# Values times probabilities with a head's high and low values side by side as the weights

## The chip, the cores and the metric

The kernel runs as one program on one core of a Trainium2 chip. The metric is the device time of one execution in microseconds (us), lower is better. TensorE (PE) does the matrix products, its weight loads have rows of their own (PEld), and VectorE (DVE), ScalarE (ACT) and GpSimd (POOL) do the element-wise work. SyncE (SP) and POOL issue the transfers.

## The reference

Two transformer blocks in float32 on 512 tokens of width 1024, one after the other. Cut to the order of the stages and to the attention on which the change bears:

```python
def first_block(x, ...):                       # one layer
    x = x + 0.5 * _swiglu(_rms_norm(x), w1, w3, w2)
    proj = _rms_norm(x) @ w_in                 # q, k, v of 8 heads of 64, and HGRN2
    attn_out = _dilated_attention(aq, ak, av)  # three windows (128,1) (512,4) (2048,16)
    rec = _hgrn2(hq, hf, hi, lower_bounds)     # chunkwise recurrence, f = lb + (1-lb)*sigmoid
    x = x + concat([attn_out, rec]) @ w_out
    return x + 0.5 * _swiglu(_rms_norm(x), ...)

def hybrid_mixer(h, ...):                      # in each of two layers of the second block
    o_cmp, p_cmp = cmp_attention(q, kc_c, vc_c)            # compressed keys and values
    o_sel = sel_attention(q, ks, vs, select_blocks(p_cmp)) # 8 heads, 2 groups of values
    o_win = win_attention(q, kw, vw)
    o_attn = g[0] * o_cmp + g[1] * o_sel + g[2] * o_win
    return concat([o_attn, short_conv(u, bg, cg, conv_w)]) @ w_o

# each attention ends in  o = einsum(p, v),  p = softmax(scores)
# second block: mixer, layer_norm, swiglu (layer 0) or an 8-expert MoE (layer 1), layer_norm
```

## The kernel before

The stages run one after the other: a feed-forward (0 to 390 us), the first block's mixer `mix1` (to 730), a feed-forward (to 1110), the second block's mixer `mix2` of layer 0 (to about 1375), a feed-forward (to 1850), `mix2` of layer 1 (to about 2080) and the experts (to 2650).

To keep float32 accuracy each operand of a product is split in a high part and a low part, both of the matmul's type (helper `cut`: ACT writes the high part, L417, and DVE subtracts it to get the low one, L418). `mm3` then does three matmuls into one PSUM tile: high by high (L429), low by high (L430) and high by low (L431).

An attention unit (`unit`) is one head's scores, softmax and product with the values for all 512 queries. PE multiplies queries and keys (L943, L944), DVE and ACT do the maximum and the exponential, POOL scales the exponentials (tile `ex`, L963), PE transposes them (L975) into the tile `ps_t`, `cut` splits them (tiles `pr`), and then come the products with the values, four of them, over 512, 256, 128 and 384 queries, each an `mm3` into `hd["o"]`, a PSUM tile `ps_o` of 128 rows by 512 queries. There are 8 units in `mix1` and 16 in each of the two `mix2`. The weights of such a product are 128 columns of values, those of two heads or groups side by side. A head's own values give 64 of the 128 rows; the other 64 are not read. At a head's close (`close` in `mix1`, the compressed products L1564 in `mix2`) `cut` takes the head's 64 rows out of `ps_o` into the tiles `mix`, `nat` or `tok`. In `mix2` two units (selected and window) and the compressed product add up in the same `ps_o`, so there are 8 closes in each mixer. The operands of L1564 are the compressed probabilities and the weights `vst`.

The order of the instructions on each engine is settled when the program is built. Generators such as `unit`, `hgrn` and `finish_v` yield a PE cost and a lag at each step; the planner `flow` picks who goes next by these estimates, and mixes the attention with other products (`ps_mm<-act`: projections and the convolution's weights; `ps_mm<-tok` and `ps_s<-tok`: the output projection of heads that are closed). On the chip every engine then works through its list in that order, and waits where a semaphore is not there yet.

`clear` zeroes two buffers in DRAM, `xs` and `ys`, which the experts use much later. It runs once, in `mix1`: POOL fills a tile with zeros (L1115) and issues 13 transfers (L1119, L1125, L1129) from its own queue. `hgrn` is the recurrence; its step 1 - f runs on POOL (L1008), and DVE and PE's transposes (L1044) come after it.

## Time and profile before

| | |
|---|---|
| time, median of 3 runs (lowest to highest) | 2662.02 us (2652.87 to 2662.17) |
| the profiled execution: time / span | 2650.37 us / 2648.7 us |
| busy share of the span: PE / DVE / ACT / POOL | 95% / 61% / 45% / 36% |
| granted TensorE clock, mean | 0.974 |
| PE instructions | 14302 matmuls, 14302 weight loads |

A matmul's row has its start and a modelled length; neighbouring rows overlap, so what a matmul costs PE is the distance from its start to the next one's. A row of the timeline ends with the idle time of its engine just before it, and what ended that.

### The profile page before, as it was taken

The page shows a single profiled execution, that of the slowest core. Times are in us where ns is not written, and L with a number is a line of the kernel's source. Part 1 is how long each engine was busy: PE and PEld are TensorE (multiplying, and loading weights), DVE is VectorE, ACT ScalarE, POOL GpSimd, SP SyncE. Part 2 cuts the span into 40 slices and gives each one's busy share as a digit, 9 for nine tenths or more (in the row PEclk, how much of TensorE's full clock was granted, in tenths as well). Part 3 has the DMA queues.
Part 4 walks back from the last instruction along what each step waited for, and adds up shares of the span by engine and source line. Part 5 has one row for each costly group of instructions (what it writes and reads, how often), then busy time and mean ns, then how long its engine had stood idle before and what let it go on. Part 6 is the DMA issues. An engine that isn't in the chain of part 4 may idle for free. (4 is left out here: it accounts for less than half of the span.)

```text
span 2648.7 us, 39980 instructions
## 1 busy us (share of the span) xinstructions
PE 2515.8 (95%) x14302; PEld 2180.2 (82%) x14302; DVE 1616.7 (61%) x3288; ACT 1191.6 (45%) x2179; POOL 965.3 (36%) x939
## 2 busy tenths in 40 slices
PE   8999999969999999999999999999999698999985
PEld 7888889858888887898888888889888597979884
DVE  6434455738754344686775323358776787799876
ACT  4222245535532222365544222235554276777763
POOL 4222222423122322433233222243332336767873
PEclk9999999979899999999999999999999898999997
DMA  4232232382032322241112232233211289799981
GB/s 161 81 110 96 74 117 80 99 185 77 24 99 79 110 96 74 94 136 63 58 41 80 81 107 100 75 107 103 82 60 46 73 301 330 262 369 324 332 309 69
DMA packets 103771, 342.06 MB, mean 129 GB/s; under 512 B 11984, under 2 KB 12800, under 8 KB 103568
## 3 DMA queue, kind: packets, MB, share of 16 engines
q1 hardware_dynamic: 95472, 311.58, 34.5%
q0 software_dynamic: 8096, 27.87, 4.0%
q8 instruction: 115, 1.88, 0.3%
q14 instruction: 88, 0.72, 0.1%
HBM read 316.59 MB, written 22.81 MB: 128 GB/s over the span
## 5 line engine op out<-in xcount | busy, mean ns | idle before, releaser
L282 POOL TENSOR_TENSOR w_lo<-w_raw,w_hi 128x224 fp32r<-128x224 f32 (+2 forms) x578 | 671.3, 1168 | 1153.6 <-ACT w_hi L276 1083.3
L276 ACT CAST w_hi<-w_raw 128x1024 fp32r<-128x1024 f32 (+3 forms) x615 | 600.5, 981 | 868.8 <-issue 243.2
L280 DVE TENSOR_TENSOR w_lo<-w_raw,w_hi 128x800 fp32r<-128x800 f32 (+5 forms) x616 | 653.3, 1067 | 301.0 <-ACT w_hi L276 294.4
L430 PE MATMUL ps_mm<-act_lo,w_hi 128*128 128x512 f32 (+1 forms) x784 | 304.0, 388 | 0.7 <-DVE act_lo L418 0.7
L429 PE MATMUL ps_mm<-act_hi,w_hi 128*128 128x512 f32 (+1 forms) x784 | 304.2, 389 | 0.0
L431 PE MATMUL ps_mm<-act_hi,w_lo 128*128 128x512 f32 (+1 forms) x784 | 303.3, 387 | 0.0
L429 PE MATMUL ps_s<-act_hi,w_hi 128*128 128x512 f32 (+1 forms) x456 | 174.6, 383 | 6.8 <-ACT w_hi L279 6.8
L963 POOL TENSOR_SCALAR ex<-ex,st 128x512 f32<-128x512 f32 (+3 forms) x160 | 90.0, 574 | 233.3 <-DVE st L960 151.3
L430 PE MATMUL ps_s<-act_lo,w_hi 128*128 128x512 f32 (+1 forms) x456 | 174.1, 382 | 0.0
L431 PE MATMUL ps_s<-act_hi,w_lo 128*128 128x512 f32 (+1 forms) x456 | 173.8, 381 | 0.4 <-DVE w_lo L280 0.4
L431 PEld LDWEIGHTS ps_mm<-act_hi,w_lo 128*128 128x128 f32 x784 | 149.2, 190 | 29.4
L430 PEld LDWEIGHTS ps_mm<-act_lo,w_hi 128*128 128x128 f32 x784 | 148.8, 190 | 28.8 <-DVE act_lo L418 1.0
L429 PEld LDWEIGHTS ps_mm<-act_hi,w_hi 128*128 128x128 f32 x784 | 148.3, 189 | 28.2
L429 PE MATMUL ps_mm<-w_hi,act_hi 128*128 128x256 f32 (+1 forms) x544 | 156.5, 288 | 7.0 <-DVE nat L1252 3.2
L431 PE MATMUL ps_mm<-w_hi,act_lo 128*128 128x256 f32 (+1 forms) x544 | 155.5, 286 | 0.2 <-DVE act_lo L634 0.2
L430 PE MATMUL ps_mm<-w_lo,act_hi 128*128 128x256 f32 (+1 forms) x544 | 154.9, 285 | 0.0
L955 ACT ACTIVATE ex<-ex,st 128x512 f32<-128x512 f32 (+3 forms) x160 | 89.7, 562 | 62.7 <-DVE st L953 62.4
L429 PEld LDWEIGHTS ps_mm<-w_hi,act_hi 128*128 128x128 f32 x544 | 103.0, 189 | 8.7 <-DVE nat L1252 3.6
L429 PEld LDWEIGHTS ps_s<-act_hi,w_hi 128*128 128x128 f32 x456 | 86.3, 190 | 24.3 <-ACT w_hi L279 6.8
L430 PEld LDWEIGHTS ps_mm<-w_lo,act_hi 128*128 128x128 f32 x544 | 103.1, 190 | 0.7 <-DVE w_lo L280 0.2
L431 PEld LDWEIGHTS ps_mm<-w_hi,act_lo 128*128 128x128 f32 x544 | 102.9, 189 | 0.9 <-DVE act_lo L634 0.5
L1700 PE MATMUL ps_s<-x_cut,w_hi 128*128 128x288 f32 x288 | 78.5, 353 | 25.3 <-DVE x_cut L418 14.2
(702 smaller groups left out, 6344.4 us busy)
## 6 DMA issues: line engine op xcount, KB each, us to landing
w_raw<-ffn_a SPq DMA_DIRECT2D x131, 512.0 KB, 3.6
w_raw<-moe_x SPq DMA_DIRECT2D x128, 512.0 KB, 6.3
w_raw<-moe_a SPq DMA_DIRECT2D x88, 512.0 KB, 6.8
w_raw<-ffn_b SPq DMA_DIRECT2D x48, 384.0 KB, 3.0
w_raw<-ffn_b SPq DMA_DIRECT2D x48, 320.0 KB, 2.8
w_raw<-m_conv SPq DMA_DIRECT2D x24, 512.0 KB, 3.7
w_raw<-moe_b SPq DMA_DIRECT2D x32, 384.0 KB, 3.2
w_raw<-win_n SPq DMA_DIRECT2D x20, 512.0 KB, 4.4
```

The lines of the kernel that those rows point to most:

```text
L276: self.late(self.nc.scalar.copy(hi, src))
L280: self.nc.vector.tensor_tensor(lo[:, :n - m], src[:, :n - m], hi[:, :n - m].bitcast(F32), ALU.subtract)
L282: self.nc.gpsimd.tensor_tensor(lo[:, n - m:], src[:, n - m:], hi[:, n - m:].bitcast(F32), ALU.subtract)
L429: mm(out, l[0], r[0], start=first, stop=False)
L430: mm(out, l[0], r[1], start=False, stop=False)
L431: mm(out, l[1], r[0], start=False, stop=last)
L955: nc.scalar.activation(s, s, AF.Exp, bias=st[:, o:o + 1], scale=-1.0, accum_out=st[:, 2 + o:3 + o])
L963: nc.gpsimd.tensor_scalar(ex[i], ex[i], st[:, 4 + o:5 + o], 1.0, ALU.mult, ALU.mult)
L1700: nc.tensor.matmul(ps[:, :2 * CAP], w[k][0], src[:, k], start=k == 0, stop=False)
```

## The change

The values' high and low parts are stored side by side: a tile of 256 columns holds high and low of the first head (or group), then low and high of the second (`value_cols`). The weights of a product are now the 128 columns of one head, high and low. Two matmuls, one for the high and one for the low part of the probabilities, replace the three of `mm3`. A head's 64 rows of `ps_o` then hold the high values' part, and the other 64 rows the low values' part. `joined_rows` adds them at the close: ACT copies the other half to the head's rows of a tile `t`, DVE adds the head's own half, and `cut` works from `t`. The compressed values `vst` get the same width, with zeros in the other half. In `mix1` the values are written in two halves (`put_v`). In `mix2` the constant `b2v` is no longer loaded ahead, but into a `t` tile from POOL's queue inside `finish_v`. Line numbers of later lines move up by 12 to 16.

```diff
+    def value_cols(self, v):
+        v = v.rearrange("p (n c) -> p n c", c=64)
+        return v[:, 0:4:3], v[:, 1:3]
+
+    def joined_rows(self, out, o, s):
+        nc = self.nc
+        rs, other = slice(s * 64, s * 64 + 64), slice(64 - s * 64, 128 - s * 64)
+        t = self.t()
+        nc.scalar.copy(t[rs], o[other])
+        nc.vector.tensor_tensor(t[rs], t[rs], o[rs], ALU.add)
+        self.cut(out[0][rs], out[1][rs], t[rs])
...
         for j in (0, 2, 3, 1):
-            self.mm3(hd["o"][:, j * P:], vals(j), probs[j], first and j == 0, last and j == 1)
-            yield 3 * mm_us((4 - j) * P), 0.0
+            for i, p in enumerate(probs[j]):
+                nc.tensor.matmul(hd["o"][:, j * P:], vals(j), p, start=first and j == 0 and i == 0,
+                                 stop=last and j == 1 and i == 1)
+            yield 2 * mm_us((4 - j) * P), 0.0
...
-                    self.cut(mx[m][0][rs], mx[m][1][rs], hd["o"][rs])
+                    self.joined_rows(mx[m], hd["o"], s)
...
-                    hi, lo, s = av[j][0][:, t], av[j][1][:, t], norm.col[:, t:t + 1]
-                    nc.scalar.activation(hi, ps, AF.Copy, scale=s)
-                    nc.vector.scalar_tensor_tensor(lo, ps, s, hi.bitcast(F32), ALU.mult, ALU.subtract)
+                    s = norm.col[:, t:t + 1]
+                    for i in range(2):
+                        hi, lo = self.value_cols(av[j][i][:, t])
+                        v = ps[:, i * P:(i + 1) * P].rearrange("p (n c) -> p n c", c=64)
+                        nc.scalar.activation(hi, v, AF.Copy, scale=s)
+                        nc.vector.scalar_tensor_tensor(lo, v, s, hi.bitcast(F32), ALU.mult, ALU.subtract)
...
-                                     lambda j: (vals[br][0][:, j], vals[br][1][:, j]),
+                                     lambda j: vals[br][:, j, g * P:(g + 1) * P],
...
             def finish_v(s):
+                b2v = self.t(P)
+                nc.gpsimd.dma_start(b2v, a["m_b2v%d" % l])
...
-                nc.tensor.matmul(o, vst, pt[:96], start=False, stop=True)
-                rs = slice(g * 64, g * 64 + 64)
+                nc.tensor.matmul(o, vst[:, g * P:(g + 1) * P], pt[:96], start=False, stop=True)
...
-                self.cut(mx[m][0][rs], mx[m][1][rs], o[rs])
+                self.joined_rows(mx[m], o, g)
```

PE, at the first head's products in `mix1` (`pr` probabilities, `nat` values; the other rows are other work that the planner put between), before:

```order
2674 L430 MATMUL ps_o<-pr,nat 128x512
2675 L431 MATMUL ps_o<-pr,nat 128x512
2676 L429 MATMUL ps_o<-pr,nat 128x256
2677 L430 MATMUL ps_o<-pr,nat 128x256
2678 L431 MATMUL ps_o<-pr,nat 128x256
2679 L429 MATMUL ps_o<-pr,nat 128x128
2680 L943 MATMUL ps_s<-q 128x256
2681 L944 MATMUL ps_s<-q 128x256
2682 L430 MATMUL ps_o<-pr,nat 128x128
2683 L431 MATMUL ps_o<-pr,nat 128x128
```

The same head on PE after the change:

```order
2624 L1002 MATMUL ps_o<-pr,nat 128x512 x2
2625 L1002 MATMUL ps_o<-pr,nat 128x256 x2
2626 L490 MATMUL ps_t<-c_ident,rs_y 128x128 x2
2627 L1002 MATMUL ps_o<-pr,nat 128x128 x2
```

Each product has two matmuls instead of three, and other work stands between them: the planner's choices have moved.

POOL in `mix1`, around the clear, before (`w_lo`: low parts of weights; four L963 rows scale one head):

```order
68 L963 TENSOR_SCALAR ex<-ex,st 128x512
69 L963 TENSOR_SCALAR ex<-ex,st 128x384
70 L963 TENSOR_SCALAR ex<-ex,st 128x256
71 L963 TENSOR_SCALAR ex<-ex,st 128x128
72 L282 TENSOR_TENSOR w_lo<-w_raw,w_hi 128x224
73 L1115 MEMSET t 128x512
74 L1119 DMA xs<-t 576x1x512 x7
75 L1119 DMA ys<-t 672x1x512 x3
76 L1125 DMA ys<-t 128x1x512
77 L1129 DMA ys<-t 16x1x32 x2
78 L1008 TENSOR_SCALAR t<-nat 128x256 x2
79 L963 TENSOR_SCALAR ex<-ex,st 128x512
```

POOL around the clear after the change (the four L975 rows end the scaling of the fourth head):

```order
85 L975 TENSOR_SCALAR ex<-ex,st 128x512
86 L975 TENSOR_SCALAR ex<-ex,st 128x384
87 L975 TENSOR_SCALAR ex<-ex,st 128x256
88 L975 TENSOR_SCALAR ex<-ex,st 128x128
89 L282 TENSOR_TENSOR w_lo<-w_raw,w_hi 128x224 x2
90 L1129 MEMSET t 128x512
91 L1133 DMA xs<-t 576x1x512 x7
92 L1133 DMA ys<-t 672x1x512 x3
93 L1139 DMA ys<-t 128x1x512
94 L1143 DMA ys<-t 16x1x32 x2
95 L1022 TENSOR_SCALAR t<-nat 128x256 x2
96 L282 TENSOR_TENSOR w_lo<-w_raw,w_hi 128x224 x2
```

The clear stood behind the first head's scaling and ahead of the second's. It now stands behind the fourth's, and directly ahead of the recurrence's two steps (L1022, L1008 before) for the second half of its heads.

PE near the end of `mix2` of layer 0, where the planner's last `ps_mm<-act` product stands, after the change:

```order
6533 L431 MATMUL ps_mm<-act_hi,w_lo 128x512
6534 L955 MATMUL ps_s<-k_9338,q 128x512
6535 L955 MATMUL ps_s<-k_9338,q 128x384
6536 L429 MATMUL ps_mm<-tok,w_hi 128x512
6537 L430 MATMUL ps_mm<-tok,w_hi 128x512
6538 L431 MATMUL ps_mm<-tok,w_lo 128x512
```

After the last `ps_mm<-act` row the values' products of five units are still to come (their first rows are 6561, 6577, 6604, 6626 and 6642). Before, the last such row was 6709, right behind unit 12's products, and the products of three units came after it (first rows 6739, 6781 and 6795). Layer 1 moves in the same way.

## Rows read from the trace of the kernel before

**Rows 1.** The page, busy time of the engines.

```profile
PE 2515.8 (95%) x14302; PEld 2180.2 (82%) x14302; DVE 1616.7 (61%) x3288; ACT 1191.6 (45%) x2179; POOL 965.3 (36%) x939
```

**Rows 2.** Busy time by stretch: us of each engine, (x instructions), granted clock, DMA share, GB/s.

```profile
520.00:620.00 100.00, 74.73 (x543) 70.50 (x542) 48.41 (x126) 41.84 (x90) 19.47 (x30) 0.86 0.74 164
...
1180.00:1345.00 165.00, 165.00 (x948) 143.22 (x946) 121.67 (x372) 86.05 (x211) 49.64 (x71) 1.00 0.21 68
...
2022.00:2045.00 23.00, 19.35 (x121) 16.19 (x120) 16.09 (x57) 11.56 (x32) 5.37 (x10) 1.00 0.09 28
```

**Rows 3.** The values' matmuls, mean durations and counts: mix2, then mix1.

```profile
L431 PE MATMUL ps_o<-pr,vl x128: 272/318/403, 1179.9 to 2041.0; 128*128 128x512 f32 x32, 128*128 128x256 f32 x32, 128*128 128x128 f32 x32, 128*128 128x384 f32 x32
...
L431 PE MATMUL ps_o<-pr,nat x32: 273/308/402, 524.7 to 716.2; 128*128 128x512 f32 x8, 128*128 128x256 f32 x8, 128*128 128x128 f32 x8, 128*128 128x384 f32 x8
```

**Rows 4.** PE's timeline (start, length) in unit 12's values' products, mix2 layer 0.

```profile
1344.31 0.39 PE L431 MATMUL ps_o<-pr,vl 128*128 128x512 f32 x1
1344.54 0.28 PE L429 MATMUL ps_o<-pr,vh 128*128 128x256 f32 x1
...
1344.78 0.28 PE L431 MATMUL ps_o<-pr,vl 128*128 128x256 f32 x1
1344.90 0.23 PE L429 MATMUL ps_o<-pr,vh 128*128 128x128 f32 x1
...
1345.07 0.28 PE L431 MATMUL ps_o<-pr,vl 128*128 128x128 f32 x1
1345.18 0.40 PE L429 MATMUL ps_o<-pr,vh 128*128 128x384 f32 x1
...
1345.60 0.34 PE L431 MATMUL ps_o<-pr,vl 128*128 128x384 f32 x1
1345.77 0.40 PE L943 MATMUL ps_s<-k,q 128*128 128x512 f32 x1
```

**Rows 5.** Timeline: the last close of mix2 layer 0, and PE behind two other closes.

```profile
1367.07 0.58 ACT L417 CAST tok<-ps_o 64x512 fp32r<-64x512 f32 x1 [2.55 <-PE ps_o L1564]
1367.68 0.69 DVE L418 TENSOR_TENSOR tok<-ps_o,tok 64x512 fp32r<-64x512 f32 x1 [2.43 <-ACT tok L417]
...
1367.70 0.50 PE L429 MATMUL ps_mm<-tok,w_hi 128*128 128x512 f32 x1 [0.67 <-ACT tok L417]
...
717.25 0.50 PE L429 MATMUL ps_s<-nat,w_hi 128*128 128x512 f32 x1 [0.67 <-ACT nat L417]
...
2042.25 0.50 PE L429 MATMUL ps_mm<-tok,w_hi 128*128 128x512 f32 x1 [0.67 <-ACT tok L417]
```

**Rows 6.** PE's timeline in layer 1: second matmul of unit 12, first of unit 15.

```profile
2018.77 0.39 PE L430 MATMUL ps_o<-pr,vh 128*128 128x512 f32 x1
...
2038.95 0.48 PE L429 MATMUL ps_o<-pr,vh 128*128 128x512 f32 x1
```

**Rows 7.** POOL's timeline around the clear.

```profile
513.53 1.47 POOL L282 TENSOR_TENSOR w_lo<-w_raw,w_hi 128x224 fp32r<-128x224 f32 x1 [3.57 <-ACT w_hi L276]
...
515.76 4.78 POOL L1119 DMA_DIRECT2D xs<-t  x7 [0.30 <-POOL t L1115]
520.25 0.99 POOL L1119 DMA_DIRECT2D ys<-t  x1
527.70 0.67 POOL L1119 DMA_DIRECT2D ys<-t  x1 [6.46 <-DMA xs<-t]
535.85 0.67 POOL L1119 DMA_DIRECT2D ys<-t  x1 [7.48 <-DMA xs<-t]
...
562.34 0.78 POOL L1008 TENSOR_SCALAR t<-nat 128x256 f32<-128x256 f32 x2
```

**Rows 8.** PE's timeline: the first head's values' product, and the second head's transposes.

```profile
523.52 0.48 PE L429 MATMUL ps_o<-pr,nat 128*128 128x512 f32 x1
...
564.41 0.69 PE L975 MATMUL ps_t<-c_ident,ex 128*128 128x128 f32 x2 [25.27 <-POOL ex L963]
```

**Rows 9.** DMA issues: times issued, KB each, median us from issue to landing.

```profile
xs<-t POOLq DMA_DIRECT2D x7, 1152.0 KB, 40.3
...
ys<-t POOLq DMA_DIRECT2D x3, 1344.0 KB, 68.0
```

More of the change, by code (lines that the diff above doesn't have):

```diff
@@ L1225, in head @@
                 yield 0.9, 3.08
-                cs = slice(m % 2 * P, m % 2 * P + P)
-                rs = slice(s * 64, s * 64 + 64)
+                cs = slice(s * P, s * P + P)
                 def close():
@@ L1233, in close @@
                         mx.extend((both[0][:, i], both[1][:, i]) for i in range(2))
-                    self.cut(mx[m][0][rs], mx[m][1][rs], hd["o"][rs])
-                yield from self.unit(rp, hd, lambda: k, bias, None,
-                                     lambda t: (av[j][0][:, t, cs], av[j][1][:, t, cs]),
+                    self.joined_rows(mx[m], hd["o"], s)
+                yield from self.unit(rp, hd, lambda: k, bias, None, lambda t: av[j][m % 2][:, t, cs],
                                      True, True, [], [turn[n - 1]] if n else [], turn[n], [v_ev[j]], fin[n], close)
@@ L1364, in mix2 @@
             b2k = self.load("m_b2k%d" % l, pool=mc)
-            b2v = self.load("m_b2v%d" % l, pool=mc)
             ctap = self.load("m_taps%d" % l, pool=mc)
@@ L1373, in mix2 @@
             kvn = [tokens() for _ in range(4)]
-            vals = [(mc.tile([P, 4, P], F32R, name="vh%d" % i), mc.tile([P, 4, P], F32R, name="vl%d" % i))
-                    for i in range(2)]
+            vals = [mc.tile([P, 4, 2 * P], F32R, name="v%d" % i) for i in range(2)]
             both = [mc.tile([P, 2, S + 32 * br], F32R, name="k%d" % br) for br in range(2)]
@@ L1379, in mix2 @@
             nc.vector.memset(kst.bitcast(F32), 0.0)
-            vst = mc.tile([96, P], F32R, name="vst")
+            vst = mc.tile([96, 2 * P], F32R, name="vst")
+            nc.vector.memset(vst.bitcast(F32), 0.0)
             mx = []
@@ L1399, in out @@
                         self.copy(kvn[j][:, t], ps[:, :P])
-                        self.cut(vals[j - 2][0][:, t], vals[j - 2][1][:, t], ps[:, P:256])
+                        self.cut(*self.value_cols(vals[j - 2][:, t]), ps[:, P:256].rearrange("p (g c) -> p g c", g=2))
                 return out
@@ L1480, in finish_v @@
                 nc.vector.tensor_tensor(vb, ps, b2v[:96], ALU.add)
-                nc.scalar.copy(vst, vb)
-                nc.vector.tensor_tensor(vst[64:96], vb[64:96], vst[64:96].bitcast(F32), ALU.subtract)
+                vb, vs = vb.rearrange("p (g c) -> p g c", g=2), self.value_cols(vst)[0]
+                nc.scalar.copy(vs, vb)
+                nc.vector.tensor_tensor(vs[64:96], vb[64:96], vs[64:96].bitcast(F32), ALU.subtract)
                 yield 1.3, 0.0
```

## Prediction

> **What bounds the kernel now.** I read the page first, then busy time by stretch, then the waits of PE and POOL in the mixers, and the timelines there. PE is busy for 95% of the span and VectorE for 61% [rows 1], so a matmul that goes saves its time wherever PE has no idle time. The stretches show where that is. From 1180 to 1345 us, in the second mixer of layer 0, PE is busy for all of 165 us [rows 2]: there the saving counts in full. In two other places it does not. In the first mixer, from 520 to 620 us, PE works 74.73 of 100 us at a mean granted clock of 0.86 with the DMA engines 0.74 busy [rows 2], and one wait makes up the loss: PE stood 25.27 us until 564.41 for the scaling of the second head's exponentials on POOL [rows 8]. POOL was late because the clear stood ahead of it: its first transfer was issued at 515.76, several of the last five each waited for an earlier one to land, as the 6.46 and 7.48 us show, and POOL went on at 562.34 [rows 7]. The second place is the end of `mix2` in layer 1: from 2022 to 2045 PE works 19.35 of 23 us [rows 2], because there are no other products left to fill in while a unit runs through its chain of scores, exponential, scaling, transposes and split.
>
> **What goes.** The third matmul of a product costs PE the distance to the next start: for 512 columns 1344.54 - 1344.31 = 0.23 us, for 256 columns 0.12, for 128 columns 0.11 and for 384 columns 0.17 [rows 4], together 0.63 us a unit. There are 128 third matmuls in the two `mix2` and 32 in `mix1` [rows 3], four to a unit, so 32 and 8 units: 20.2 and 5.0 us, 25.2 in all, if PE were full everywhere. Reckoned by the median 318 ns of a row [rows 3] it would be 160 x 0.318 = 51 us, but lengths of neighbours overlap, and I take the starts. The weight loads that go lie beside other matmuls and are in these distances.
>
> **What comes.** A close gets one ScalarE copy of 64x512 and one VectorE add more. The rows nearest to them are the cast of 0.58 and the subtraction of 0.69 on the same 64 rows [rows 5]. A copy is the cast's kind of work, and the add reads the same shapes, so I take 0.6 + 0.7 = 1.3 us a close; bounds are 0.6 for both (a form faster than the rows) and 2.0. In 24 closes that is 17 us of VectorE and 14 us of ScalarE. In the middle of a mixer both have room beside a full PE: 121.67 and 86.05 of 165 us [rows 2]. If that cover were gone, each close would cost PE its 1.3. At the three ends nothing covers it. The PSUM tile itself comes free after the add, at the same count of one ScalarE and one VectorE step as before, so the next head does not wait longer for it. PE's next row waits for the first cast, 0.67 us at 717.25, 1367.70 and 2042.25 [rows 5]; the copy and the add now stand ahead of that cast. I put in 0.6 to 1.3 for each end and take 0.6 in the sums below, since the output projection has rows of other heads that the planner can put there. The wider value stores of `mix1` (8 more small ScalarE and 8 VectorE steps), the zeros of `vst` and the late load of `b2v` I put at nothing: full PE work covers them, and without the cover each is one step of under 0.7 us.
>
> **The tails of `mix2`.** The planner starts units by its lags, not by the time that PE has saved, so its filler runs out earlier: after the last `ps_mm<-act` row five units are left instead of three. With little filler the pace of units is that of their chain. Layer 1 before shows it: from unit 12 to unit 15 it took 2038.95 - 2018.77 = 20.18 us for three [rows 6], 6.73 each, with VectorE busy 16.09 of 23 us [rows 2]. PE's work in that stretch, counted from the order by the distances above (0.108 for 128 columns or fewer), is 17.8 us, so 2.4 were idle. In the changed order PE's work from unit 10 to unit 15, the same count, is 28.7 us in layer 0 and 25.5 in layer 1. At 6.73 a unit, five take 33.6: PE would stand 4.9 us in layer 0 and 8.1 in layer 1. Less what stood idle before (some 0.5 and the 2.4), plus 0.6 for the end, this gives -10.1 + 4.4 + 0.6 = -5.1 and -10.1 + 5.7 + 0.6 = -3.8 us: **-8.9 for both**. The pace is the uncertain part. At 6.0 a unit, as if the chains overlapped better, the two give -8.7 and -7.4, -16; at 7.4, with the add's 0.7 in every unit, -1.7 and -0.4, -2. I take 6.73 since it is the measured pace.
>
> **The clear in `mix1`.** This step decides the first mixer. In the changed order the clear stands behind the scaling of the fourth head, so the second head no longer waits for it: 25.27 us of idle time go. But right behind the clear now stand the recurrence's 1 - f rows, and PE's transposes for them. When does it start? The two `w_lo` rows ahead of it split weights whose tile PE must first be done with. From the first head's values' product (523.52 before [rows 8], 5.3 us earlier now because the planner has put less PE work ahead of it, 500.3 for 505.6 us by the same count: 518.2) to PE's last use of that tile the order has 43.8 us of PE work: 562.0. Cast, `w_lo` and fill take about 4 more (513.53 to 515.76 for `w_lo` and fill [rows 7], and a cast ahead), so it starts near 566. It holds POOL for 562.34 - 515.76 = 46.6 us [rows 7], to 612.6; about 2 us for the steps behind, and PE goes on at 614.8. PE reaches these transposes after 68.6 us of work, at 586.8. The new stall is 28.0 us, 2.7 more than the old. Of the 5.0 us of products in `mix1` the first four heads' 2.5 stay saved. The last four stand in a stretch that waits on their chains, and I take 1.0 of theirs. A later step of the recurrence on ScalarE now waits until every transfer of the clear has landed, because it reuses the zeros' tile; transfers take 40.3 and 68.0 us to land in the median [rows 9], and the last lands some 88 us after the start, near 654, about when PE needs that step. I put 2 us there, and 0.6 for the end: -2.5 - 1.0 + 2.7 + 2 + 0.6 = **+1.8**. Bounds: a clear that starts 12 us earlier takes the stall down to 16, -10; one that starts 10 us later, or a longer wait of ScalarE, +12.
>
> The Trainium skill, in DMA: Bandwidth & Descriptors, section Anatomy of one DMA, fits a transfer issued from GpSimd as 2.0 us plus its bytes over 436 GB/s. That is an estimate of 4.7 us for 1152 KB, so the whole clear would last some 30 us. By that rule POOL would be held less than half as long, and the new stall would go: -24 in `mix1` and not +1.8. The trace does not agree: POOL's waits of 6.46 and 7.48 us between late issues are what these transfers take here [rows 7], and I use them.
>
> **Sum.** -8.9 + 1.8 = -7.1 us. The profiled execution took 2650.37 with a span of 2648.7; it is the lowest of the times shown, 11.65 under the median of 2662.02. Laid on it the change gives 2643.3, on the median 2654.9, and I forecast **2655**.
>
> **Rivals.**
> 1. *The whole gain arrives, or more.* For it: PE is the full engine. It comes about if the clear starts 12 us earlier, which needs only that the weight tile comes free earlier than my count, and the tails keep a pace of 6.0: -16 - 10 = -26, 2636. The plain rule that PE is the bound gives -25, 2637. Against it: two of three mixer ends are not bounded by PE. A faster clear, 46.6 us of POOL cut to half, belongs here too: the stall falls to 4 us, `mix1` gives -22 and the sum is up to -38, 2624; nothing in the rows speaks for it. Together 0.30.
> 2. *The small gain above*, faster or slower by less than 0.5%: 0.60.
> 3. *The clear's block lands on PE in full: slower.* If it starts when PE arrives, the stall is 46.6 + 2 and not 28: +23 in `mix1`, and with -8.9 from the tails +14, 2676. The point from which it decides is a start at about 587, 21 us later than my 566; it needs POOL to fall behind in the fourth head's scaling or ScalarE to hold the weight cast. For it: POOL waited 3.57 us for a cast just before the clear [rows 7]. Against it: the tile's release stands well ahead. Chance 0.10.
>
> **How the numbers follow.** 0.5% is 13 us, about what a measurement of this kernel can tell from no change: faster is under 2649, slower over 2675. Rival 1 puts 0.30 below 2649; the forecast has 0.60, and rival 3 0.10. The forecast's own bounds are -16 - 10 = -26 and -2 + 12 = +10; the ends of both together are rare. The range 2634 to 2672 takes rival 1 in but for a shorter clear, and leaves about 0.2 out: 0.1 for rival 3, and 0.1 below and between.
>
> **What would show it.** 14142 PE matmuls, 160 fewer, and distances in a product unchanged. The wait of 25 us for the second head's scaling gone, and one of 16 to 31 us at the recurrence's transposes behind POOL's clear, some 45 us later in the trace. Tails with five units at 6 to 7.4 us apart and new idle time of PE for the split of probabilities or a scaling. ScalarE and VectorE with 24 more 64x512 rows each of about 0.6 and 0.7 us. I am wrong if the clear starts before 555 or after 580, if another wait in `mix1` opens, or if the five units keep up with PE.

## The result, and the profile after

The changed kernel took 2677.70 us, the median of 6 runs (2671.32 to 2687.96), and the kernel before 2656.34 in as many. The ratio is 1.0084 (95% interval 1.0065 to 1.0103): 22 us slower, where 7 faster were forecast. The profiled execution took 2675.99, 25.6 more than that of before.

The page of the changed kernel (span, busy time):

```profile
span 2673.9 us, 39761 instructions
...
PE 2510.6 (94%) x14142; PEld 2167.4 (81%) x14142; DVE 1645.1 (62%) x3322; ACT 1214.7 (45%) x2217; POOL 961.2 (36%) x939
```

The 160 matmuls are gone, but PE is busy for only 5 us less [rows 1]; VectorE has 28 us more, ScalarE 23. Busy time by stage (columns as in [rows 2]), `mix1` from 390 us with the feed-forward behind it, `mix2` of layer 0, `mix2` of layer 1, each to the first row of the next stage; first before, then after:

```profile
390.00:1106.86 716.86, 681.11 (x3876) 589.54 (x3874) 392.33 (x799) 277.29 (x492) 191.36 (x189) 0.97 0.33 93
1106.86:1390.16 283.30, 278.47 (x1781) 249.41 (x1782) 213.13 (x604) 150.97 (x360) 97.16 (x131) 0.99 0.22 71
1781.74:2088.55 306.81, 289.38 (x1879) 258.31 (x1880) 224.22 (x663) 157.95 (x374) 90.92 (x125) 0.99 0.24 80
```

```profile
390.00:1127.30 737.30, 685.89 (x3862) 593.77 (x3860) 406.44 (x823) 290.88 (x514) 183.80 (x189) 0.95 0.32 91
1127.30:1413.89 286.59, 273.62 (x1718) 240.84 (x1719) 221.82 (x612) 156.24 (x368) 99.28 (x131) 0.99 0.22 70
1805.80:2113.90 308.10, 284.51 (x1815) 250.91 (x1816) 232.09 (x671) 163.29 (x382) 92.94 (x125) 0.98 0.24 79
```

The three stages are 20.4, 3.3 and 1.3 us longer: 25.0 of the 25.6. To split this, I took the same view in windows of 5 us: idle is what PE is not busy, the clock's part is busy time times one less the granted clock, and the rest is work.

| | idle | clock | work | length |
|---|---|---|---|---|
| `mix1`, before to after | 35.8 to 51.4 | 10.7 to 19.2 | 670.4 to 666.7 | +20.4 |
| `mix2` layer 0 | 4.8 to 13.0 | 1.7 to 2.7 | 276.8 to 270.9 | +3.3 |
| `mix2` layer 1 | 17.4 to 23.6 | 0.0 to 2.6 | 289.4 to 282.0 | +1.3 |

So the work did shrink, by 17 us of the 25.2 forecast. Idle time grew by 30 us, and 12 more came from a lower granted clock. The waits of PE name the idle time (us in all, times, longest):

```profile
PE ps_t L1058 <- DVE t L1045: 32.6, 2, 32.4
...
PE ps_t L1573 <- DVE c L1569: 7.7, 4, 4.0
...
PE ps_mm L429 <- DVE nat L1267: 4.6, 3, 3.2
PE ps_o L429 <- DVE t L928: 4.2, 3, 1.4
PE ps_t L429 <- ACT r L417: 3.9, 2, 2.4
```

The first takes the place of the 25.27 us of [rows 8]. L1573 transposes the compressed probabilities of a head in `mix2`; L928 is the join's add. Before, PE waited 1.1 us in all for compressed heads, and there was no add to wait for. POOL around the clear, then PE's first head's product and its stall:

```profile
575.76 4.78 POOL L1133 DMA_DIRECT2D xs<-t  x7 [0.30 <-POOL t L1129]
...
587.72 0.67 POOL L1133 DMA_DIRECT2D ys<-t  x1 [6.48 <-DMA xs<-t]
...
622.12 0.78 POOL L1022 TENSOR_SCALAR t<-nat 128x256 f32<-128x256 f32 x2
```

```profile
483.84 0.33 PE L429 MATMUL ps_t<-r 128*128 128x128 f32 x1 [2.41 <-ACT r L417]
...
487.52 0.55 PE L429 MATMUL ps_mm<-w_hi,act_hi 128*128 128x256 f32 x1 [3.24 <-DVE nat L1267]
...
527.12 0.94 PE L1002 MATMUL ps_o<-pr,nat 128*128 128x512 f32 x4
...
629.16 0.66 PE L1058 MATMUL ps_t<-c_ident,t 128*128 128x128 f32 x2 [32.40 <-DVE t L1045]
```

POOL was held for 622.12 - 575.76 = 46.4 us, as in [rows 7]. The clear began 10 us later than forecast, since the first head's product came at 527.12 and not at 518.2: PE had stood 2.41 and 3.24 us on its way there, where its longest wait before was 1.8.

Where a join stands in the tail of `mix2`, layer 1 (ScalarE, VectorE and PE):

```profile
2053.35 0.58 ACT L927 COPY t<-ps_o 64x512 f32<-64x512 f32 x1
2053.95 0.59 ACT L417 CAST pr<-ps_t 128x512 fp32r<-128x512 f32 x1
...
2053.96 0.68 DVE L928 TENSOR_TENSOR t<-t,ps_o 64x512 f32<-64x512 f32 x1
2054.57 0.69 DVE L418 TENSOR_TENSOR pr<-ps_t,pr 128x512 fp32r<-128x512 f32 x1
...
2060.14 0.29 DVE L1569 TENSOR_TENSOR c<-t,c 128x128 fp32r<-128x128 f32 x1 [0.42 <-ACT c L1567]
...
2060.58 1.06 PE L1573 MATMUL ps_t<-c_ident,c 128*96 128x128 f32 x4 [3.95 <-DVE c L1569]
```

The copy stands ahead of the cast of another unit's probabilities, the add ahead of their subtraction, and behind those follow the steps of the compressed head for which PE waits 3.95 us. From the add at 2053.96 to 2057.65 VectorE has a single gap, of 0.25 us. So here the join has no idle engine to go to: it is one more link in a chain.

A fact of the program that the section on the kernel before leaves out: the planner `flow` gives the instructions, but a scheduler of the framework (`schedule_with_timeline_sim=True` in the kernel) then puts them in order once more. Where the clear stands depends on free `t` tiles, and each join takes one: in e18 below, without joins, POOL issues the clear at 516.54, behind the first head, though the call stands where the changed kernel has it. Small edits therefore move rows far away from them, and the experiments have to be read with that in mind.

### The profile page after: what moved, and what is told of

Read it like the earlier page. It is cut to its first block, busy times and chain, and to the rows that moved or that the text cites. A ratio compares the mean times of both kernels' runs of the same rounds, so it can differ in the third digit from the quotient of the medians.

```text
span 2673.9 us, 39761 instructions
## 1 busy us (share of the span) xinstructions
PE 2510.6 (94%) x14142; PEld 2167.4 (81%) x14142; DVE 1645.1 (62%) x3322; ACT 1214.7 (45%) x2217; POOL 961.2 (36%) x939
## 5 line engine op out<-in xcount | busy, mean ns | idle before, releaser
L282 POOL TENSOR_TENSOR w_lo<-w_raw,w_hi 128x224 fp32r<-128x224 f32 (+2 forms) x578 | 661.4, 1151 | 1199.6 <-ACT w_hi L276 1077.5
L280 DVE TENSOR_TENSOR w_lo<-w_raw,w_hi 128x800 fp32r<-128x800 f32 (+5 forms) x616 | 654.8, 1069 | 299.1 <-ACT w_hi L276 293.1
L975 POOL TENSOR_SCALAR ex<-ex,st 128x512 f32<-128x512 f32 (+3 forms) x160 | 97.4, 622 | 223.4 <-DVE st L970 106.9
L967 ACT ACTIVATE ex<-ex,st 128x512 f32<-128x512 f32 (+3 forms) x160 | 89.5, 560 | 42.9 <-DVE st L965 42.1
```

What stands on the lines that cost most here:

```text
L280: self.nc.vector.tensor_tensor(lo[:, :n - m], src[:, :n - m], hi[:, :n - m].bitcast(F32), ALU.subtract)
L282: self.nc.gpsimd.tensor_tensor(lo[:, n - m:], src[:, n - m:], hi[:, n - m:].bitcast(F32), ALU.subtract)
L967: nc.scalar.activation(s, s, AF.Exp, bias=st[:, o:o + 1], scale=-1.0, accum_out=st[:, 2 + o:3 + o])
L975: nc.gpsimd.tensor_scalar(ex[i], ex[i], st[:, 4 + o:5 + o], 1.0, ALU.mult, ALU.mult)
```

## The experiments

Ratios are to the kernel before on the same chip, with their 95% interval; windows have the columns of [rows 2].

**1. The split value stores.** In the changed kernel `put_v` went back to one ScalarE and one VectorE step (a tile then holds high and low of each of four heads); and the kernel before got stores in two halves and nothing else.

```diff
# e1, changed kernel
-                    for i in range(2):
-                        hi, lo = self.value_cols(av[j][i][:, t])
+                    w = tokens(j, t).rearrange("p (n k c) -> p n k c", n=4, k=2)
+                    hi, lo, v = w[:, :, 0], w[:, :, 1], ps.rearrange("p (n c) -> p n c", c=64)
# e2, kernel before
+                    for i in range(2):
+                        hi, lo, v = (x[:, i * P:(i + 1) * P] for x in (av[j][0][:, t], av[j][1][:, t], ps))
```

> The changed kernel, but the values of the first mixer are again written by one ScalarE and one VectorE instruction a token tile, not by two each (all four heads of a token tile lie in one tile, high beside low). PE's order up to the first head's products is then that of the kernel before; the clear still stands behind the fourth head. Theory A, that the split stores set off the reordering that cost the stretch ahead of the first head some 9 us: 8 to 10 us less than the changed kernel, near +0.5% on the kernel before, and the idle time of 2.4 and 3.2 us at 484 and 487 us gone. Rival, that the stores are at nothing as the prediction had it and the loss there comes with the products or the joins: within 3 us of the changed kernel, +0.8%.

> The kernel before with that one part of the change alone: each store of values in the first mixer in two halves, 8 more ScalarE and 8 more VectorE instructions, products, joins and clear as before. Theory A: about 9 us slower than the kernel before, +0.3%, with the first head's products near 527 us and not 523.5. Rival (at nothing): within 3 us, 0.0% to +0.1%.

e2 took 2668.92, ratio 1.0046 (1.0030 to 1.0063): 12 us for an edit that was put at nothing. It shows the two early waits, and a longer stall:

```profile
481.58 0.47 PE L429 MATMUL ps_t<-r 128*128 128x128 f32 x1 [2.41 <-ACT r L417]
...
485.26 0.55 PE L429 MATMUL ps_mm<-w_hi,act_hi 128*128 128x256 f32 x1 [2.98 <-DVE nat L1254]
...
568.47 0.48 PE L975 MATMUL ps_t<-c_ident,ex 128*128 128x128 f32 x1 [31.21 <-POOL ex L963]
```

So these waits belong to the stores. But e1, without them, took 2675.06, 1.0080 (1.0059 to 1.0100): nothing came back. Its early waits are gone and its stall is 24.77, but 7.2 us at a low part of the activations are new. The stores cost alone, and their removal does not pay in the changed order.

**2. The clear, in fewer transfers.** 6 larger transfers for 13, in each kernel.

```diff
-        put(self.xs[CAP:SLOTS], 6)
-        put(self.ys[(NE - 1) * CAP:ZERO_ROW], 7)
+        put(self.xs[CAP:SLOTS], 21)
+        put(self.ys[(NE - 1) * CAP:ZERO_ROW], 21)
```

> The changed kernel with the same bytes cleared by 6 transfers instead of 13, so that POOL has none to wait for, at the same place in its list. Theory A, that POOL's 46 us behind the clear are what holds PE for 32 us at the recurrence's transposes: 25 to 32 us less than the changed kernel, 0.97% below it, about -0.1 to -0.3% on the kernel before. Rival B, that the traffic itself (DMA engines at 0.9 busy) or the zeros' tile holds the next steps: less than 10 us gained, another wait of 20 us or more in the same place.

> The kernel before with the clear in 6 transfers instead of 13 at the same place. Theory A: the wait of 25 us for the second head's scaling goes, 22 to 28 us less than the kernel before, -0.9 to -1.0%, and the change against this kernel costs 0 to 10 us more than its own products save in the tails. Rival B (traffic or tile): less than 10 us gained.

The changed kernel took 2675.13, 1.0064 (1.0041 to 1.0087), that of before 2657.88, 1.0009 (0.9994 to 1.0025). POOL was free at 521.65 in the latter, and PE stood all the same, for steps of the recurrence. Behind them is a product on VectorE (L1034) that waits for the clear's transfers, since it writes the zeros' tile again:

```profile
607.78 0.43 DVE L1034 TENSOR_TENSOR t<-nat,t 128x256 f32<-128x256 f32 x1 [27.24 <-DMA ys<-t]
```

```profile
609.58 0.48 PE L429 MATMUL ps_t<-r 128*128 128x128 f32 x1 [24.44 <-ACT r L417]
```

In the changed kernel it was 28.00 us, behind a step on ScalarE that waits in the same way:

```profile
664.61 1.28 ACT L1041 ACT_TABLE_LOAD   x1 [32.48 <-DMA ys<-t]
```

The issuing of transfers is not the cost; the tile that they hold until they land costs the same.

**3. The clear from a tile of its own,** of 1 KB a partition, in 8 transfers; it then stands at the start of `mix1` (at 386.42 us in the kernel before).

```diff
-    def clear(self):
-        zero = self.t()
+    def clear(self, zero):
...
-            self.clear()
+            self.clear(mc.tile([P, HALF], F32, name="zero"))
```

> The kernel before with the clear in 8 transfers and from a tile of zeros of its own (1 KB a partition), so that neither POOL nor the next user of a shared tile waits for the transfers; it then stands at the start of the first mixer. Theory A, that the clear costs PE one stall of some 25 us wherever it stands, on POOL's queue or on the shared tile: 20 to 26 us less than the kernel before, -0.8 to -1.0%. Rival, that its traffic of some 88 us delays the weights there: within 8 us of the kernel before.

> The changed kernel with the same clear from a tile of its own. Theory A: the stall of 32 us goes here too; what stays against the kernel with that clear and without the change is the split stores' reordering ahead of the first head (9 us) and the tails of the second mixers, +10 to +18 us on it, so about -0.2 to -0.5% on the kernel before. Rival, that the first mixer's loss is in the order of heads and recurrence and not in the clear: 0 to -10 us against the changed kernel, +0.4 to +0.8%.

2645.33, 0.9961 (0.9948 to 0.9975) for the kernel before, 2649.98, 0.9980 (0.9969 to 0.9991) with the change. The 25 us of stall are worth 10 here, which neither expectation had. In the profiled execution, the slowest of its six with 2649.22, `mix1` with its feed-forward is 716.64 long (idle 25.7, clock 18.9), no shorter than in the one of before: 10 us of idle time went and 8 came back by the clock. With the stall away the changed kernel is 4.7 us behind the other, and the intervals touch: here the change costs some 5 us and not 22.

**4. The two mixers apart.** The change in `mix2` alone; that without the joins, which takes the rows with the high values only and leaves the low ones out; and the change in `mix1` alone.

```diff
# e7: mix1 as before
+            if gate is None:
+                self.mm3(hd["o"][:, j * P:], vals(j), probs[j], first and j == 0, last and j == 1)
# e8: e7, and
-                self.joined_rows(mx[m], o, g)
+                self.cut(mx[m][0][rs], mx[m][1][rs], o[rs])
# e9: mix2 as before
+            if gate is not None:
```

> The change in the two second mixers alone; the first mixer is that of the kernel before, PE's whole order up to there too. Theory A, that the filler ends early and the last five units run at the pace of their chain, 7.6 to 7.8 us each: the 20 us of products are eaten, +3 to +7 us, +0.1 to +0.3%. Rival, that the losses of the second mixers in the changed kernel come from the first one's state: -9 to -17 us, -0.3 to -0.6%.

> As the kernel with the change in the second mixers alone, but the close takes the high values' half only and leaves the sum of the halves out (no copy, no add), so 16 ScalarE and 16 VectorE instructions fewer. Theory B, that the joins in the chains of the tail units set their pace: 8 to 16 us less than with the joins. Theory A, that the pace is that of scores, exponential, scaling and split, and joins cost their 1.3 us at the two ends and little between: 1 to 5 us less.

> The change in the first mixer alone, split stores, products in two and joins, with the clear as in the changed kernel; the second mixers are those of the kernel before. Theory A, that the stages add: 0.84% less the 0.28% of the second mixers, so +0.5 to +0.6%, 13 to 16 us slower than the kernel before. Rival, that the first mixer's loss is given back later: under +0.3%.

e7 took 2664.08, 1.0028 (1.0014 to 1.0041); e8 2647.54, 0.9970 (0.9957 to 0.9983). So leaving out 16 joins saves 16.5 us, about 1 us each. Windows of e7, then of e8, in layer 1: up to unit 10's products, the tail from there to unit 15's, and from there to the end.

```profile
1789.03:2007.35 218.32, 212.63 (x1357) 190.31 (x1358) 171.91 (x466) 123.31 (x286) 75.21 (x99) 0.99 0.25 82
2007.35:2049.81 42.46, 34.79 (x190) 28.68 (x188) 32.12 (x113) 24.30 (x67) 11.68 (x22) 0.88 0.08 28
2049.81:2100.73 50.92, 40.60 (x272) 35.11 (x273) 29.18 (x94) 16.34 (x31) 5.14 (x5) 0.90 0.27 101
```

```profile
1777.93:1995.14 217.21, 212.84 (x1358) 190.78 (x1358) 167.25 (x471) 120.10 (x285) 71.20 (x101) 0.99 0.25 83
1995.14:2032.58 37.44, 33.69 (x190) 27.69 (x188) 29.44 (x105) 22.13 (x61) 10.98 (x19) 0.95 0.09 32
2032.58:2081.30 48.72, 38.85 (x271) 33.47 (x272) 27.65 (x88) 15.65 (x30) 5.15 (x5) 0.92 0.30 105
```

Both tails have 190 matmuls. With joins units come 42.46/5 = 8.5 us apart, without them 7.5, with 2.7 us more of VectorE work, 3.9 more idle time of PE and a granted clock of 0.88 for 0.95. In layer 0 the tails are 39.77 and 36.49 long, with 4.85 and 1.75 idle. Up to unit 10, where five of the eight closes lie, idle time is only 1.3 us more with joins (5.69 for 4.37; in layer 0 5.91 for 4.45), behind unit 15 0.4 to 0.6. So the joins' idle time lies mostly in the tails, and the middle of these mixers nearly covers them. Over both layers and the feed-forward between them idle time is 42.9 us with joins and 31.5 without (29.2 in the kernel before), and the clock's part 14.7 and 7.2; the changed kernel, with the same joins there, has 43.5 and 8.2, so that the clock's part is not the joins' alone. PE's waits in the last two windows together, e7, then e8:

```profile
PE ps_t L1575 <- DVE c L1571: 4.9, 2, 3.9
PE ps_o L429 <- DVE t L928: 1.4, 1, 1.4
...
PE ps_o L1006 <- DVE t L928: 0.6, 1, 0.6
```

```profile
PE ps_o L1006 <- DVE tok L418: 1.4, 1, 1.4
PE ps_mm L429 <- ACT tok L417: 0.7, 1, 0.7
...
PE ps_t L1575 <- DVE c L1571: 0.6, 1, 0.6
```

The compressed head's wait falls from 4.9 to 0.6 (layer 0: from 2.8 to none), the end's from 1.4 to 0.7. The next head's wait for its PSUM tile does not fall: it is 0.6 for the add with joins, and 1.4 for the close's subtraction (`tok`, L418) without.

e9 took 2675.57, 1.0086 (1.0070 to 1.0102), as much as the whole change and more than either expectation had. The two parts, 0.86% and 0.28%, add up to more than the whole's 0.84%. Each build has its own order, and `mix1`'s stall of 36.27 us in e9 is 4 us longer than in the whole.

**5. The clear away in the first mixer's part, and VectorE relieved.** e10 is e9 with the clear of e5. e11 is e7 with the low part of the joined rows subtracted on POOL. e12 is the whole change with both.

```diff
-        self.cut(out[0][rs], out[1][rs], t[rs])
+        nc.scalar.copy(out[0][rs], t[rs])
+        nc.gpsimd.tensor_tensor(out[1][rs], t[rs], out[0][rs].bitcast(F32), ALU.subtract)
```

> The change in the first mixer alone, and the clear from a tile of its own in 8 transfers. Theory A, that the loss of the first mixer is only how its order meets the clear: the products' 5 us show, 2 to 8 us below the kernel with that clear and without the change, -0.5 to -0.7% on the kernel before. Rival, that split stores and joins cost more than the products give even without the clear: 0 to +5 us on that kernel, -0.2 to -0.4%.

> The change in the second mixers alone, with the low part at a close subtracted by POOL from SBUF and not by VectorE, so VectorE has one step a close as before the change. Theory B1, that the joins' price is VectorE's load: most of the 16 us that the joins cost come back, 6 to 14 us below the same kernel with VectorE's subtraction, -0.2 to 0.0%. Theory B2, that it is the length of the chain from the product to the output projection and to the free bank: within 4 us of it, +0.2 to +0.4%.

> The whole change with the clear from its own tile and the low part at a close on POOL. If B1 holds, -0.5 to -0.7% on the kernel before, the fastest so far; if B2 holds, as the kernel with the clear's own tile alone, -0.1 to -0.3%.

e10: 2643.05, 0.9959 (0.9945 to 0.9973), the same as e5 without the change: in `mix1` it then neither costs nor pays. e11: 2656.79, 1.0004 (0.9993 to 1.0015), 7 us below e7 (0.24% by the ratios), at the low end of what B1 expected. But PE's wait for the compressed heads is still 7.4 us there, and over both `mix2` and the feed-forward between them PE's idle time is 42.2 us for e7's 42.9; what fell in the profiled execution is the clock's part, 5.9 for 14.7. That VectorE's time for the subtraction was the price is therefore not shown. e12: 2644.12, 0.9957 (0.9941 to 0.9973). It beats both kernels and lies between its two expectations, but its gain is that of the clear, which e5 has without the change.

**6. Where the clear stands.** e13 is the kernel before with `clear` called later, so that it stands behind the fourth head as in the changed one; e15 is the changed kernel with the clear behind the first head, as before; e14 is e15 with the stores of e1.

```diff
# e13
+                    if j == 1 and i == 0:
+                        self.clear()
# e14, e15
             heads(0)
+            self.clear()
```

> The kernel before with one line moved: the clear is called later, so that it stands on POOL behind the fourth head's scaling and ahead of the recurrence's 1 - f, as in the changed kernel; products, stores and closes are those of before. Theory C, that the clear's new place is worth most of the first mixer's loss: 8 to 18 us slower than the kernel before, +0.3 to +0.7%. Theory D, that the place is indifferent (a stall of 25 to 30 us at either) and the loss is the split stores': within 5 us, -0.2 to +0.2%.

> The whole change with the values stored by one instruction pair a token tile and the clear called earlier, so that it stands behind the first head's scaling as in the kernel before. If the first mixer's loss is the clear's place and the split stores and nothing else, only the second mixers' loss is left: +0.1 to +0.3% on the kernel before. If it is the joins or the products there, +0.6 to +0.9% as the changed kernel.

> The whole change with the clear called earlier, behind the first head's scaling, and the stores split as in the change. Theory C: the clear's place is given back and the split stores' 9 us stay, +0.3 to +0.6%. Theory D: the split stores alone make the loss, as in the kernel before with split stores alone (+0.46%), plus the second mixers: +0.6 to +0.9%.

e13: 2656.83, 1.0000 (0.9989 to 1.0012). The stall is 28.48 us at another row (between the clear and 1 - f another step, L1197, stands there), and in the kernel before the place of the clear is worth nothing. e15, the changed kernel with the clear moved back: 2683.71, 1.0120 (1.0098 to 1.0142), more than both expectations had. e14, with the stores in one as well: 2674.97, 1.0075 (1.0058 to 1.0092), with the stall and the place of before:

```profile
565.70 0.48 PE L987 MATMUL ps_t<-c_ident,ex 128*128 128x128 f32 x1 [26.56 <-POOL ex L975]
```

So with the stores in one, the clear where it was and a stall 1.3 us longer than that of [rows 8], the change still costs 0.75%. What is left of it are the matmuls, the joins and the new order.

**7. All remedies together, and no joins.** e16 is e12 with the stores of e1. e17 is e14 without the joins in `mix1`, e18 the whole change without any join; both leave out one half of each sum.

```diff
# e17 (mix1), e18 (mix1 and mix2)
-                    self.joined_rows(mx[m], hd["o"], s)
+                    self.cut(mx[m][0][rs], mx[m][1][rs], hd["o"][rs])
```

> The whole change with all that the runs spoke for: the clear from its own tile, values stored by one instruction pair, the low part at a close on POOL. If the three add, 4 to 10 us below the kernel before with that clear alone, -0.5 to -0.8% on the kernel before; if the products' gain stays eaten by the joins, -0.3 to -0.5%.

> As e14 (whole change, values stored by one instruction pair, the clear behind the first head), but the closes of the first mixer take the high values' half only: their copy and add, 8 each, are left out, and the low values' part is missing from these heads. Theory J, that the joins make what is left of the first mixer's loss, as they made the second mixers': 8 to 14 us below e14, +0.2 to +0.4% on the kernel before. Rival P, that it is the shorter products, whose filler ends earlier ahead of the recurrence's chain: within 4 us of e14, +0.6 to +0.9%.

> The whole change with every join left out, 24 copies and adds; the split stores stay, and the clear stands behind the first head's scaling by itself, since the joins' tiles no longer take the room of its zeros. Theory J: the second mixers give -8 us as alone, the first has only the split stores' loss of 9 to 12: 0.0 to +0.2%. Rival P: +0.4 to +0.7%.

e16: 2660.25, 1.0021 (1.0009 to 1.0033), 16 us above e12 for fewer instructions, where both expectations had it faster than the kernel before; its first mixer has 29.2 us of clock loss, e12's 24.4. So the order that an edit brings can move this kernel by half a per cent, as much as e7 and e8 differ: one pair of kernels proves little here. In e17 the odd heads' rows hold the low values, so that the experts get other tokens; its total (3202.01, 1.2052) says nothing and only `mix1` ahead of them is read, e17 first, then e14:

```profile
390.00:1114.15 724.15, 682.84 (x3854) 590.91 (x3852) 395.31 (x802) 276.74 (x492) 190.63 (x189) 0.96 0.32 92
```

```profile
390.00:1122.61 732.61, 683.76 (x3849) 590.59 (x3848) 402.38 (x809) 280.62 (x500) 190.91 (x189) 0.95 0.31 91
```

So leaving out 8 joins saves 8.5 us. Most of it lies between the fourth and the fifth head's products (603.73 to 691.18 in e17, 603.22 to 697.47 in e14), where PE stands 7.95 and 13.34 us; of the difference 4.3 us are one wait of e14 for a weight's low part on VectorE (L280), which e17 does not have.

e18: 2656.83, 1.0000 (0.9990 to 1.0010): without its 24 joins the changed kernel is as fast as the one before. That is 22 us below the changed kernel, 0.9 a join, and 27 below e15, whose clear stands where that of e18 does, 1.1 a join. It is not faster than the kernel before, although a third of the products' matmuls is gone. It still has the split stores, and its `mix1` with the feed-forward is 10 us longer than before, with the early waits of e2 (2.41 and 2.99 us) and a stall of 30.22 us:

```profile
390.00:1116.95 726.95, 680.54 (x3842) 588.21 (x3840) 392.86 (x808) 284.65 (x505) 188.13 (x189) 0.96 0.32 92
```

```profile
485.28 0.55 PE L429 MATMUL ps_mm<-w_hi,act_hi 128*128 128x256 f32 x1 [2.99 <-DVE nat L1268]
...
567.49 0.90 PE L987 MATMUL ps_t<-c_ident,ex 128*128 128x128 f32 x3 [30.22 <-POOL ex L975]
```

## Why the prediction was wrong

**The step that failed** is the cover of the joins: "In the middle of a mixer both have room beside a full PE", and "At the three ends nothing covers it". By these two sentences 24 joins were charged 0.6 us at three ends, 1.8 in all. The price "If that cover were gone, each close would cost PE its 1.3" stood beside it. Measured with three kernels without joins (e8, e17, e18), they cost 0.9 to 1.1 each in either mixer, 22 to 27 us in all. The durations were right (0.58 and 0.68), the cover was not. In the second mixers the sentence on the middle nearly held: up to unit 10 five closes cost 1.3 to 1.5 us of idle time a layer. What the sum left uncharged are the tails, where two closes cost 3.1 and 3.9 us. A share of 121.67 of 165 us was read where PE has other work ready; in a tail VectorE works through its list in order, and steps for which PE waits next stand behind the join, as the rows at 2053 to 2060 show. In `mix1` half of the price is one wait on VectorE (e17 against e14); whether the join causes it, and how much of the rest comes by the clock, I did not isolate.

Two limits remain. Order alone moved this kernel by as much as one of the three pairs differs; that the pairs agree on about 1 us a join speaks against chance, but no kernel held the order fixed. And the price is no constant: with the clear on a tile of its own the whole change costs some 5 us (e6 against e5), and there no kernel without joins was run.

**The sum.** Without joins the second mixers gave 8 us (e8), where the forecast without its two ends has -8.9 - 1.2 = -10.1. With the joins at 22 for 1.8 and the split stores at 12 (e2) for nothing the sum of -7.1 becomes +25, an estimate, since parts do not add exactly here (0.86% and 0.28% for 0.84%); measured were +22.

**The matmuls**: 160 fewer, as forecast. Their distances in both `mix2`, summed from start to next start with waits left out, fell from 63.3 to 47.1 us, 16.2 of 20.2.

**The tails**: five units each, as forecast, but the pace was mis-sized, 6.73 with a bound of 7.4. From unit 10 to unit 15 the changed kernel took 1386.85 - 1348.96 = 37.89 us in layer 0 and 2063.80 - 2024.62 = 39.18 in layer 1, 7.6 and 7.8 a unit (the first rows of unit 10's and 15's products; of layer 1 they are these):

```profile
2024.62 0.83 PE L1002 MATMUL ps_o<-pr,v 128*128 128x512 f32 x3
...
2063.80 0.80 PE L1002 MATMUL ps_o<-pr,v 128*128 128x512 f32 x1
```

That is 9.8 us more than 5 x 6.73 twice. Half of it is the counting: [rows 6] start at unit 12's second matmul of 512 columns, behind other work; its first one started here:

```profile
2017.38 0.39 PE L429 MATMUL ps_o<-pr,vh 128*128 128x512 f32 x1
```

From first to first it is 21.57 us for three, 7.19 a unit, near the 7.3 and 7.5 of e8, which has no joins. With joins the changed kernel takes 7.6 and 7.8, and e7 8.0 and 8.5. PE's idle time in the five units, 5.3 and 7.9 us, is close to the 4.9 and 8.1 forecast, but by luck: without joins it is 1.75 and 3.75.

**The ends**: PE waited 1.39 us at each for the add, for 0.67 [rows 5], 0.7 more, where 0.6 was taken. "The PSUM tile itself comes free after the add ... so the next head does not wait longer for it" held: in layer 1 unit 14's first product waited 1.56 us for the close's subtraction before, and 0.61 for the add now (first before, then after):

```profile
2033.35 0.47 PE L429 MATMUL ps_o<-pr,vh 128*128 128x512 f32 x1 [1.56 <-DVE tok L418]
```

```profile
2054.79 1.84 PE L1002 MATMUL ps_o<-pr,v 128*128 128x512 f32 x8 [0.61 <-DVE t L928]
```

**The clear**: it lies behind the fourth head, holds POOL for 46.4 us, and lands on the recurrence's transposes, as forecast; the stall is 32.4 and not 28.0. Ten us of a later start were met by a later arrival of PE (596.76 for 586.8), the rest came from VectorE (below). The place that "decides the first mixer" does not decide: e13 has it and no loss. By the rule that was weighed there, of the Trainium skill, in DMA: Bandwidth & Descriptors, section Anatomy of one DMA, the clear would have held POOL less than half as long; the trace, with 46.4 us, disagrees once more.

**The split stores** "at nothing" cost 12 us in the kernel before (e2), and e18 has their two waits and a `mix1` that is 10 us longer. Their removal gave 9 us with the clear moved back (e14 against e15), nothing in the changed kernel (e1), and e16 was slower without them. How they work together with the order stays open, and so does why `mix1`'s part alone costs as much as the whole.

**The clock**: no term of the sum had it. PE's granted clock is a mean over its two levels, 1.2 and 2.4 GHz. From 680 to 735 us, some 50 us behind the stall, it was 0.98 before and is 0.84 now (first before, then after):

```profile
680.00:735.00 55.00, 51.82 (x329) 45.26 (x328) 45.72 (x111) 33.15 (x77) 11.06 (x16) 0.98 0.12 36
```

```profile
680.00:735.00 55.00, 48.94 (x256) 41.80 (x255) 41.56 (x116) 28.93 (x70) 11.40 (x18) 0.84 0.06 20
```

PE is busy for 3 us less of this stretch, in a chain of short waits. Ahead of it, from 670 to 675, PE worked 2.06 of 5 us, and from 675 to 685 the clock stood at 0.50, the lower level. Over the mixers the clock adds 12 us to 30 of idle time.

Rival 3 named nearly the time, 2676, but not for its reason: its clear would have to start at 587, and it started at 575.76, and e13 and e14 clear it of the loss. Of the prediction's own signs of being wrong one came: other waits opened in `mix1`, the 2.41 and 3.24 us.

## What to carry to other kernels

A step put ahead of a chain that PE waits for costs PE time, however free its engine is on average: where other work for PE runs out, price an added step at its full length or more (3.1 and 3.9 us of idle time for two joins of 1.3 in the tails), and look at the rows behind it before taking it as covered elsewhere. A matmul taken away pays only where PE has other work ready; of the 25 us forecast 17 showed as less work, and joins and split stores cost more than that. In a program that a scheduler orders, test each edit alone and as its own control (the split stores, the place of the clear), and in more than one pair of kernels: the order alone was worth half a per cent. A bulk transfer holds its source tile until it lands, so it wants a tile that nobody else waits for (10 us in e5).

## What the hardware showed that was not expected

VectorE's product for the recurrence, two inputs in SBUF, took 6.44 us where its group of 8 has a median of 0.43, while POOL worked on four instructions from SBUF, two of each row (VectorE, then POOL):

```profile
622.57 6.44 DVE L1045 TENSOR_TENSOR t<-t 128x256 f32<-128x256 f32 x1 [26.28 <-POOL t L1022]
```

```profile
622.87 1.27 POOL L282 TENSOR_TENSOR w_lo<-w_raw,w_hi 128x224 fp32r<-128x224 f32 x2
624.10 4.63 POOL L1211 TENSOR_TENSOR nat<-nat,c_qk_gain 128x1024 f32<-128x1024 f32 x2
```

VectorE is done at 629.01, just behind the last of these four, at 628.73, and PE goes on at 629.16. In e9 the same row takes 6.44 us again. The Trainium skill, in SBUF — State Buffer, section SBUF: two separate sides, says that VectorE with two inputs in SBUF and GpSimd share a pair of ports that one holds for a whole instruction while the other is blocked. The trace agrees in that VectorE stood while POOL worked; that it stood through four of POOL's instructions in a row is what the rows add. From POOL's release at 622.12 to PE's start it took 7.0 us, where 2 were forecast.
